# A two-layer hybrid decoder trunk on one core: first x ahead of the first weights, turns of y a pair later, other banks for the auxiliary tiles, casts behind scalings at a seam

## The chip, the core and the metric

The kernel runs on one core of a Trainium2 chip. The metric is the device time of one execution in microseconds, here the median of the runs. The profile comes from one further execution, taken by the hardware profiler. The engines are TensorE (PE in the profile; PEld is its weight load, the load of the stationary operand, which overlaps the matmuls), VectorE (DVE), ScalarE (ACT), GpSimd (POOL) and SyncE (SP), whose queue issues most of the DMA transfers.

## The reference

Two layers over 256 tokens of width 2048, all in float32. Layer 0 has one input projection of 12,336 columns, shared by an mLSTM group (8 heads) and a Mamba-2 SSD group (32 heads of 64); layer 1 is block-sparse attention, which with 256 tokens and blocks of 256 is causal attention over all. Each layer ends in a SwiGLU FFN of width 5632.

```python
def swiglu(x, w_gate, w_up, w_down):
    return (jax.nn.silu(x @ w_gate) * (x @ w_up)) @ w_down

for layer in range(DEPTH):
    xn = rms_norm(x, norm_mix[layer])
    if layer % 2 == 0:
        x = x + mixer_mlstm_ssd(xn, *mixer_params[layer])
    else:
        x = x + mixer_moba(xn, *mixer_params[layer])
    x = x + swiglu(rms_norm(x, norm_ffn[layer]), *ffn_params[layer])
return rms_norm(x, final_norm)
```

Inside `mixer_mlstm_ssd` the SSD group runs a depthwise convolution and SiLU over x, B and C, a chunked scan, and a gated group norm: `y = rms_norm(y * silu(z))` for each of the 8 groups of 256 columns. That y goes with the mLSTM output through one output projection.

## The kernel before

**Products.** Every weight matrix streams once from HBM through SBUF. A float32 product is computed as three float32r products: each operand is cut into a high part (a cast, `wh`, on ScalarE, line 252) and a low part (the difference, `wl`, on VectorE, line 257), and TensorE adds high x high, high x low and low x high (lines 288 to 290) into PSUM. "A product" below means one of these three matmuls of 128 x 512.

**Blocks and pairs.** `block` computes a tile of 256 tokens by 1024 columns. It walks over pairs of 128 contraction rows: 8 pairs for a width of 2048. For each pair, SP loads two raw tiles of 512 KB, ScalarE casts them and VectorE takes the differences. A pair marked P in the table `PLAN` takes 24 products into four accumulators `acc_f` (banks 0 to 3), in the order 0, 2, 1, 3. A pair marked S takes seven Strassen-like sums of three products, 21 instead of 24; four of the sums go into `acc_e` (banks 4, 5, 6 and 7, in the order of use: E1 in 4, E7 in 5, E5 in 6, E6 in 7). The text calls E5 the third and E6 the fourth Strassen sum. Before an S pair VectorE also builds sums of the weights, and of the activations (`sk`, from a copy `xg` of the turned activations).

**Turns.** The activations have to stand with the contraction along the partitions. A turn is four 128 x 128 transposes on TensorE into one auxiliary bank (`transpose_split`, tile `p_tr`, line 209), which ScalarE and VectorE then read to write the high and low parts. The auxiliary tiles take the banks of the list `AUX` in rotation, begun anew at each block; they share banks 4 to 7 with the Strassen sums.

**Order.** Programs for the five engines come from a scheduler that follows program order and priorities (`high_priority`) and explicit ties (`tied`, `issue_after`: an instruction may not be placed ahead of another). Small work between the products is put on a list with `later(wait, ...)` and is run `wait` pairs on, by `tick` at the end of each pair.

**Names that the change touches.** `warm_up` runs matmuls on a tile of ones at the start; `WARM` gives the calls before the turn of the first gains (`p_rows`) and after the turns of the first x (line 413). `load_x` issues the transfers of the input (`xin`, line 107), `first_pair` those of the first weights (line 407). `weights` ties its casts behind the last cast, the last difference and whatever stands in the list `also`. `bc_done` empties the accumulators of a B/C block: `scaled` (line 467) multiplies each by the norm's root into `tok`. `xz_block` (four of them, columns of x and z) does the same, and between its products the scan of the groups before it runs: `p_xs`, `p_y` (line 708), then `ssd_gate`: y is gated, squared and summed, its root is taken on GpSimd (`rrg`, line 137), ScalarE scales y (line 727), and a turn of y (line 209) is set for later. `decay_rows` (line 637) issues transfers on GpSimd's queue. The order of the blocks is: two B/C blocks, four xz blocks, the mLSTM's blocks and the output projection, the FFN of layer 0 ("a", its hidden tiles named `ha`), attention, the FFN of layer 1 ("b", `hb`).

The turns of y before:

```python
for t in range(NT):
    nc.scalar.activation(y[:, t, cs], y[:, t, cs], AF.Copy, scale=rr[:, t:t + 1])
later(1, ("sx", 2 * s + g), transpose_split, sx, 2 * s + g, [y[:, t, cs] for t in range(NT)], G_SS)
```

Of the kernel before, what the change touches and what calls it, by code (L numbers as in the profile page):

```python
# [17 lines left out]
P = 128  # L18
# [13 lines left out]
C_Q, C_K, C_V, C_O, C_I, C_F, C_Z, C_X, C_B, C_C, C_DT = (  # L32
    0, 1024, 2048, 4096, 6144, 6152, 6160, 8208, 10256, 11280, 12304)

WARM = (7, 8)
SPACE = {"raw": 6, "sum": 2, "wh": 6, "wl": 6, "xa": 8, "sk": 3, "s": 9, "vh": 2}
PLAN = {
    "bc": "PPPPPPPP", "xz": "PPPPPPPP", "qk0": "PPPPPPPP", "w1": ("PSPSPSPP", "PSPSPSPP"),
# [23 lines left out]
def hybrid_trunk(ctx: ExitStack, tc: tile.TileContext, a: dict, out: bass.AP):  # L62
# [25 lines left out]
    def tiny(shape, tag):  # L88
        return sml.tile(shape, F32, tag=tag, name=tag, bufs=2)

    turn = [0]
    AUX = (6, 7, 4, 5)

    def bank(i, name):
        return psm.tile([P, 512], F32, tag=f"b{i}", name=name)
# [3 lines left out]
        return bank(AUX[(turn[0] - 1) % len(AUX)], name)  # L99

    ones = cst.tile([P, P], F32, name="ones")
    nc.gpsimd.memset(ones, 1.0)
    xin = [big.tile([P, D], F32, tag="xr", name=f"xin{t}", bufs=2) for t in range(NT)]

    def load_x(lo, n):
        for t in range(NT):
            nc.sync.dma_start(xin[t][:, lo:lo + n], x_in[t * P:(t + 1) * P, lo:lo + n])

    load_x(0, T)
    rows = cst.tile([P, P], F32, name="rows")  # L110
    by_row = lambda nm: a[nm].rearrange("(a b) -> a b", b=P)
    ident = cst.tile([P, P], F32, name="ident")
# [37 lines left out]
            stack.enter_context(tc.issue_after(ins))  # L150
        return stack

    also = []
    last, cast, nth, fresh = [None], [None], [None], [None, None]
    clock = [0]
    held = [False]
# [13 lines left out]
    def tick():  # L170
        clock[0] += 1
        run_until(lambda p: held[0] or p[0] > clock[0])
# [31 lines left out]
    def transpose_split(kt, j, src, gcol):  # L204
        b = kt.pair(j)
        pt = aux_bank("p_tr")
        for i in range(2):
            for t in range(NT):
                turned = nc.tensor.transpose(pt[:, i * T + t * P:i * T + (t + 1) * P], src[t][:, i * P:(i + 1) * P], ident)  # L209
        pair = pt.rearrange("p (a b) -> p a b", a=2)  # L210
        gains = None if gcol is None else [pv[:, gcol + 2 * j + i:gcol + 2 * j + i + 1] for i in range(2)]
        if j in kt.sums:
            xg = t2([P, 2, T], "xg")
            if gains is None:
                nc.scalar.copy(xg, pair)
            else:
                for i in range(2):
                    nc.scalar.activation(xg[:, i, :], pair[:, i, :], AF.Copy, scale=gains[i])
            split(b[:, :, 0, :], b[:, :, 1, :], xg)
            kt.sums[j] = activation_sums(xg, kt.sum_home[j])  # L220
        elif gains is None:
            split(b[:, :, 0, :], b[:, :, 1, :], pair)
        else:
            for i in range(2):
                split(b[:, i, 0, :], b[:, i, 1, :], pair[:, i, :], gains[i])
        return turned.ins
# [52 lines left out]
    def block(src, kt, row, plan, after_sums=None, lead=1, ready=None, order=(0, 2, 1, 3),  # L279
              first_weights=None):  # L280
        n = len(plan)
        F = [None] * 4
        pre = None
        E = {}

        def add(dst, a, b, start, stop, **kw):
            (ah, al), (bh, bl) = a, b
            nc.tensor.matmul(dst, ah, bh, start=start, stop=False, **kw)  # L288
            nc.tensor.matmul(dst, ah, bl, start=False, stop=False, **kw)  # L289
            nth[0] = nc.tensor.matmul(dst, al, bh, start=False, stop=stop, **kw).ins  # L290

        first_s, last_s = plan.find("S"), plan.rfind("S")
        turn[0] = 0
        group = []
        for j in range(n):
            if plan[j] == "S":
                sk = kt.summed(j)
                held[0] = True
                b21, b11, b22, t3, t1, t2_, t4 = weights(src, row + 2 * j * P, True)
                tok = lambda k, t: tuple(x[:, t * P:(t + 1) * P] for x in kt.parts(k))  # L300
                k2, k1 = 2 * j, 2 * j + 1
                a11, a12, a22 = tok(k1, 0), tok(k2, 0), tok(k2, 1)
                s1, s2, s3, s4 = [(sk[:, i, 0, :], sk[:, i, 1, :]) for i in range(4)]
                prod = {1: (a11, b11), 2: (a12, b21), 3: (s4, b22), 4: (a22, t4),
                        5: (s1, t1), 6: (s2, t2_), 7: (s3, t3)}
                for p in (2, 1, 3, 7, 5, 6, 4):
                    if p in (2, 3, 4):
                        i = p - 2
                        fresh = F[i] is None
                        if fresh:  # L310
                            F[i] = bank(i, "acc_f")
                        add(F[i], *prod[p], start=fresh, stop=False)
                    else:
                        if p not in E:
                            E[p] = bank({1: 4, 7: 5, 5: 6, 6: 7}[p], "acc_e")
                        add(E[p], *prod[p], start=j == first_s, stop=j == last_s)
                if j == last_s:
                    pre = [t2([P, STRIP], "pre") for _ in range(4)]
                    p1, v, u3, w = pre
                    with tc.high_priority(offset=1600):  # L320
                        nc.scalar.copy(p1, E[1])
                        nc.vector.tensor_add(v, p1, E[6])
                        nc.vector.tensor_add(u3, v, E[7])
                        nc.vector.tensor_add(v, v, E[5])
                        nc.vector.tensor_add(w, u3, E[5])
                    if after_sums is not None:
                        after_sums(pre)
            else:
                group.append((j, first_weights if j == 0 and first_weights else weights(src, row + 2 * j * P, False)))
                if ready is not None:  # L330
                    ready(j, False)
                if len(group) < lead and j < n - 1 and n - j <= lead:
                    continue
                for i in order:
                    t, s = divmod(i, 2)
                    first = F[i] is None
                    if first:
                        F[i] = bank(i, "acc_f")
                    halves = (slice(0, T), slice(T, STRIP)) if lead > 1 and j == n - 1 and i == order[-1] else (slice(0, STRIP),)
                    for cs in halves:  # L340
                        apart = cs.start > 0
                        if apart:
                            F.append(bank(4, "acc_last"))
                        dst = F[4][:, :T] if apart else F[i][:, cs]
                        for jj, w in group:
                            for kk in range(2):
                                xh, xl = kt.parts(2 * jj + kk)
                                ts = slice(t * P, (t + 1) * P)
                                add(dst, (xh[:, ts], xl[:, ts]), [v[:, cs] for v in w[s][kk]],
                                    start=(first or apart) and jj == group[0][0] and kk == 0,  # L350
                                    stop=jj == n - 1 and kk == 1)
                    if ready is not None and i == 2:
                        with tc.issue_after(nth[0]):
                            ready(j, True)
                group = []
            tick()
            if j == last_s:
                held[0] = False
        return F, pre
# [104 lines left out]
    def scaled(t, src, r):  # L464
        d = t2([P, STRIP], "tok")
        with tc.high_priority(offset=1600):
            nc.scalar.activation(d, src, AF.Copy, scale=r[:, t:t + 1])  # L467
        return d

    def bc_done(s, got):  # L470
# [157 lines left out]

    settled.close()
    later(2, "gates", gate_chain)  # L630
    later(6, "gates", gate_columns)

    def decay_rows(first, home):
        need("gates")
# [14 lines left out]


    FB = bc_block(1)
    also.clear()
    bc_done(1, FB)

    sx = KT("sx", KD, s_home, {1: vh_home, 3: vh_home, 5: sk_home})
# [62 lines left out]
    def ssd_gate(s, g, y, zg):  # L718
        cs = slice(g * T, (g + 1) * T)
        nc.vector.tensor_mul(y[:, :, cs], y[:, :, cs], zg[:, :, cs])  # L720
        ssg = tiny([P, NT], "ssg")
        for t in range(NT):
            sumsq(ssg[:, t:t + 1], y[:, t, cs])
        rr = tiny([P, NT], "rrg")
        rsqrt_mean(rr, ssg, T)
        for t in range(NT):
            nc.scalar.activation(y[:, t, cs], y[:, t, cs], AF.Copy, scale=rr[:, t:t + 1])
        later(1, ("sx", 2 * s + g), transpose_split, sx, 2 * s + g, [y[:, t, cs] for t in range(NT)], G_SS)

    for s in range(4):  # L730
        xz_block(s)
# [315 lines left out]
    def finish_last(F):  # L1047
# [17 lines left out]
            dve(nc.vector.tensor_scalar, so_far[t], so_far[t], 1.0 / D, EPS, op0=OP.mult, op1=OP.add)  # L1065

        def root(t, n):
            rf[t] = tiny([P, 1], "rf")
            dve(nc.vector.scalar_tensor_tensor, rf[t], ssf[t][:, n:n + 1], 1.0 / D, so_far[t], op0=OP.mult, op1=OP.add)
            with tc.high_priority(offset=1600):  # L1070
                nc.gpsimd.tensor_tensor(rf[t], rf[t], mhalf[:, :1], op=OP.pow)

        def scale(t, cs, queue, on_scalar=False):
            x = xr_[t]
# [59 lines left out]
```

## Time and profile before

| what | value |
|---|---|
| median of 3 runs | 2576.79 us (2576.51 to 2577.45) |
| the profiled execution | 2576.37 us, span 2574.6 us |
| granted TensorE clock, mean of the span | 0.999 |
| TensorE busy | 2558.9 us, 99% of the span |
| VectorE, ScalarE, GpSimd busy | 87%, 58%, 2% |
| DMA | 494.52 MB, 192 GB/s on average |

The timeline's rows give the start, the busy time, the engine, the line, the operation, what it writes and reads, and in brackets how long the engine stood before it and for what. A product's row has 0.39 us, but products are pipelined: what counts is the distance from one start to the next. "PE p_tr L209 <- ACT y L727: 2.9, 5, 0.7" in the list of waits says that matmuls of the tile p_tr of line 209 waited five times for the ScalarE instruction of line 727 on y, 2.9 us in all and 0.7 at the longest.

### The profile page before, as it was taken

What the parts mean: (1) busy time and instruction counts of PE and PEld (TensorE: products, weight loads), DVE (VectorE), ACT (ScalarE), POOL (GpSimd) and SP (SyncE); (2) the same over time, 40 slices, a digit from 0 to 9 for tenths busy, and PEclk for the clock granted to TensorE, in tenths of its full rate; (3) what the DMA queues carried; (4) which work ended last, traced back from release to release, by engine and by line L of the source; (5) the groups of instructions that cost most, each with busy time, mean ns of one, the idle gap of its engine ahead of it and who ended that gap; (6) DMA issues with size and microseconds to landing.
All of it is one profiled execution on the core that took longest, in us unless ns stands there. A gap on an engine that the chain in (4) does not pass through costs nothing.

```text
span 2574.6 us, 32831 instructions
## 1 busy us (share of the span) xinstructions
PE 2558.9 (99%) x11699; PEld 2110.6 (82%) x11699; DVE 2238.3 (87%) x3027; ACT 1504.7 (58%) x2032; POOL 63.6 (2%) x106
## 2 busy tenths in 40 slices
PE   9999999999999999999999999999999999999998
PEld 7888888888888888888888888888888888888887
DVE  5777789877799999999999988978899999999998
ACT  6566666565666555555555655656565555554554
POOL 2001110000000000000000000000000000000000
PEclk9999999999999999999999999999999999999999
DMA  8556666656566666665666656555556666656664
GB/s 270 171 175 181 189 172 206 198 176 212 164 193 190 204 188 214 188 212 182 218 186 207 193 184 193 176 164 179 176 176 197 194 205 191 204 189 228 195 203 142
DMA packets 255699, 494.52 MB, mean 192 GB/s; under 512 B 16120, under 2 KB 18688, under 8 KB 255536
## 3 DMA queue, kind: packets, MB, share of 16 engines
q1 hardware_dynamic: 251088, 482.08, 59.8%
q0 software_dynamic: 3264, 8.51, 1.5%
q8 instruction: 92, 1.51, 0.2%
q10 hardware_dynamic: 1184, 1.84, 0.2%
q14 instruction: 71, 0.58, 0.1%
HBM read 490.23 MB, written 2.14 MB: 191 GB/s over the span
## 4 chain that ended last, share of the span: by engine, by line
PE 93%; issue 4%; POOL 1%; DVE 1%; ACT 0%; DMA 0%; SPq 0%; POOLq 0%; DVEq 0%; ACTq 0%
PE acc_f L288 25%; PE acc_f L290 25%; PE acc_f L289 25%; PE acc_e L288 5%; PE acc_e L290 5%; PE acc_e L289 5%; PE p_tr L209 1%; POOL rows L637 0%; PE p_qt L753 0%; PE p_num L796 0%; PE p_o L1010 0%; PE p_qk L982 0%; PE p_y L708 0%; PE p_pt L1001 0%; DVE wl L257 0%
## 5 line engine op out<-in xcount | busy, mean ns | idle before, releaser
L252 ACT CAST wh<-raw 128x1024 fp32r<-128x1024 f32 (+1 forms) x1038 | 1023.1, 999 | 830.6 <-PE acc_f L290 578.2
L257 DVE TENSOR_TENSOR wl<-raw,wh 128x1024 fp32r<-128x1024 f32 (+1 forms) x1038 | 1186.8, 1155 | 233.3 <-ACT wh L252 231.3
L288 PE MATMUL acc_f<-wh,x 128*128 128x512 f32 x1336 | 524.1, 392 | 0.0
L290 PE MATMUL acc_f<-wh,x 128*128 128x512 f32 x1336 | 521.5, 390 | 0.0
L289 PE MATMUL acc_f<-wl,x 128*128 128x512 f32 x1336 | 521.3, 390 | 0.0
L290 PEld LDWEIGHTS acc_f<-wh,x 128*128 128x128 f32 x1336 | 250.8, 188 | 52.2
L289 PEld LDWEIGHTS acc_f<-wl,x 128*128 128x128 f32 x1336 | 251.2, 188 | 51.2
L288 PEld LDWEIGHTS acc_f<-wh,x 128*128 128x128 f32 x1336 | 250.9, 188 | 50.9
L288 PE MATMUL acc_f<-wh,xa 128*128 128x512 f32 x708 | 281.8, 398 | 0.7 <-ACT tok L467 0.7
L290 PE MATMUL acc_f<-wh,xa 128*128 128x512 f32 x708 | 277.6, 392 | 0.0
L289 PE MATMUL acc_f<-wl,xa 128*128 128x512 f32 x708 | 276.8, 391 | 0.0
L257 DVE TENSOR_TENSOR wl<-sums,wh 128x1024 fp32r<-128x1024 f32 x128 | 156.1, 1220 | 11.9 <-ACT wh L252 11.9
L290 PEld LDWEIGHTS acc_f<-wh,xa 128*128 128x128 f32 x708 | 133.2, 188 | 28.0
L288 PEld LDWEIGHTS acc_f<-wh,xa 128*128 128x128 f32 x708 | 133.4, 188 | 26.4 <-ACT tok L467 0.9
L289 PEld LDWEIGHTS acc_f<-wl,xa 128*128 128x128 f32 x708 | 133.3, 188 | 26.2
L288 PE MATMUL acc_e<-wh,sk 128*128 128x512 f32 x384 | 152.7, 398 | 0.0
L289 PE MATMUL acc_e<-wl,sk 128*128 128x512 f32 x384 | 150.1, 391 | 0.0
L290 PE MATMUL acc_e<-wh,sk 128*128 128x512 f32 x384 | 149.9, 391 | 0.0
L252 ACT CAST wh<-sums 128x1024 fp32r<-128x1024 f32 x128 | 134.0, 1047 | 21.0 <-PE acc_f L290 10.5
L367 DVE TENSOR_TENSOR pre<-pre,acc_f 128x512 f32<-128x512 f32 x152 | 102.6, 683 | 6.3 <-PE acc_f L290 4.0
L288 PE MATMUL acc_f<-wh,ha 128*128 128x512 f32 x262 | 102.4, 391 | 0.0
L290 PE MATMUL acc_f<-wh,ha 128*128 128x512 f32 x262 | 102.0, 389 | 0.0
(339 smaller groups left out, 3725.1 us busy)
## 6 DMA issues: line engine op xcount, KB each, us to landing
raw<-in_l_w_in SPq DMA_DIRECT2D x192, 512.0 KB, 4.2
raw<-in_l_ffn_gate SPq DMA_DIRECT2D x176, 512.0 KB, 4.4
raw<-in_l_ffn_up SPq DMA_DIRECT2D x176, 512.0 KB, 4.4
raw<-in_l_ffn_down SPq DMA_DIRECT2D x176, 512.0 KB, 4.8
raw<-in_l_w_qkv SPq DMA_DIRECT2D x96, 512.0 KB, 4.4
raw<-in_l_w_out SPq DMA_DIRECT2D x64, 512.0 KB, 4.6
raw<-in_l_w_o SPq DMA_DIRECT2D x32, 512.0 KB, 3.8
rows<-scr POOLq DMA_DIRECT2D x20, 256.0 KB, 5.5
```

The source lines that it names most:

```text
L209: turned = nc.tensor.transpose(pt[:, i * T + t * P:i * T + (t + 1) * P], src[t][:, i * P:(i + 1) * P], ident)
L252: cast[0] = nc.scalar.copy(h[:, :n, :], of[:, :n, :]).ins
L257: last[0] = nc.vector.tensor_sub(l[:, :n, :], of[:, :n, :], h[:, :n, :].bitcast(F32)).ins
L288: nc.tensor.matmul(dst, ah, bh, start=start, stop=False, **kw)
L289: nc.tensor.matmul(dst, ah, bl, start=False, stop=False, **kw)
L290: nth[0] = nc.tensor.matmul(dst, al, bh, start=False, stop=stop, **kw).ins
L367: nc.vector.tensor_add(pre[i], pre[i], F[i])
```

## The change

Eight edits, the last without effect on the order:

1. The second warm-up has 4 calls instead of 8.
2. `AUX` begins with bank 7, then 6.
3. The memset of ones and the first transfer of x get a high priority.
4. The transposes of a turn are tied behind the last product placed so far (`nth[0]`).
5. At the block behind one whose accumulators are scaled (`scaled`), the weights of the third pair are tied behind the last scaling (`evacuated`), and the ties in `also` end with the first pair of that block instead of its last.
6. The gates' columns are set seven pairs on instead of six.
7. The turns of y are set two pairs on instead of one.
8. The last norm's mean has a tile of its own.

```diff
-WARM = (7, 8)
+WARM = (7, 4)
...
-    AUX = (6, 7, 4, 5)
+    AUX = (7, 6, 4, 5)
...
-    nc.gpsimd.memset(ones, 1.0)
+    with tc.high_priority(offset=4000):
+        nc.gpsimd.memset(ones, 1.0)
...
-    load_x(0, T)
+    with tc.high_priority(offset=4000):
+        load_x(0, T)
...
-    also = []
+    also, evacuated = [], []
...
         pt = aux_bank("p_tr")
-        for i in range(2):
-            for t in range(NT):
-                turned = nc.tensor.transpose(...)
+        with tied(nth[0]):
+            for i in range(2):
+                for t in range(NT):
+                    turned = nc.tensor.transpose(...)
...
             else:
+                if j == 2 and evacuated:
+                    also[:] = evacuated
                 group.append((j, first_weights if j == 0 and first_weights else weights(src, row + 2 * j * P, False)))
...
                 group = []
+            if ready is None and evacuated:
+                also.clear()
             tick()
...
         with tc.high_priority(offset=1600):
-            nc.scalar.activation(d, src, AF.Copy, scale=r[:, t:t + 1])
+            evacuated[:] = [nc.scalar.activation(d, src, AF.Copy, scale=r[:, t:t + 1]).ins]
...
-    later(6, "gates", gate_columns)
+    later(7, "gates", gate_columns)
...
     FB = bc_block(1)
-    also.clear()
...
-        later(1, ("sx", 2 * s + g), transpose_split, sx, 2 * s + g, [y[:, t, cs] for t in range(NT)], G_SS)
+        later(2, ("sx", 2 * s + g), transpose_split, sx, 2 * s + g, [y[:, t, cs] for t in range(NT)], G_SS)
...
-            rf[t] = tiny([P, 1], "rf")
-            dve(nc.vector.scalar_tensor_tensor, rf[t], ssf[t][:, n:n + 1], 1.0 / D, so_far[t], op0=OP.mult, op1=OP.add)
+            rf[t], mean = tiny([P, 1], "rf"), tiny([P, 1], "mean_f")
+            dve(nc.vector.scalar_tensor_tensor, mean, ssf[t][:, n:n + 1], 1.0 / D, so_far[t], op0=OP.mult, op1=OP.add)
             with tc.high_priority(offset=1600):
-                nc.gpsimd.tensor_tensor(rf[t], rf[t], mhalf[:, :1], op=OP.pow)
+                nc.gpsimd.tensor_tensor(rf[t], mean, mhalf[:, :1], op=OP.pow)
```

The rows below are the scheduled order of an engine's instructions (line, operation, what it writes and reads, shape, how many in a row). The changed kernel's lines stand a few lines further down: 107, 209, 252, 407, 467 and 708 become 108, 212, 255, 414, 474 and 714.

SP's queue at the start of the program, before (xin are the tiles of the input, raw the weights):

```order
L407 DMA raw<-in_l_w_in 128x2x512 x2
L107 DMA xin_78<-in_x 128x256
L107 DMA xin_79<-in_x 128x256
L107 DMA xin_78<-in_x 128x256
L107 DMA xin_79<-in_x 128x256
```

And after:

```order
L108 DMA xin_78<-in_x 128x256
L108 DMA xin_79<-in_x 128x256
L414 DMA raw<-in_l_w_in 128x2x512 x2
L108 DMA xin_78<-in_x 128x256
L108 DMA xin_79<-in_x 128x256
```

The first two transfers of x have moved ahead of the two first weight transfers; what follows them stays. On GpSimd's queue the memset of ones has moved ahead of one of a weight tile.

ScalarE at the seam between the first and the second block, before (xa are the turned inputs of the first block's last pair, tok the scalings, rb a copy for the gates):

```order
L144 ACTIVATE xa_444<-p_tr,pv 128x256 x2
L252 CAST wh<-raw 128x1024 x6
L467 ACTIVATE tok<-acc_f,r_544 128x512 x4
L521 COPY rb_555<-p_rb 128x256
L252 CAST wh<-raw 128x1024 x2
```

And after:

```order
L146 ACTIVATE xa_440<-p_tr,pv 128x256 x2
L255 CAST wh<-raw 128x1024 x4
L474 ACTIVATE tok<-acc_f,r_540 128x512 x4
L255 CAST wh<-raw 128x1024 x2
L528 COPY rb_551<-p_rb 128x256
```

Two of the six casts have moved behind the four scalings. On VectorE one difference (line 257) has moved behind dg (line 518), and on TensorE p_rb now stands ahead of the turn p_rows.

TensorE in the second xz block, at a turn of y, before (xa_444 are the inputs of a pair; the products go on above and below):

```order
L288 MATMUL acc_f<-wh,xa_444 128x512
L289 MATMUL acc_f<-wl,xa_444 128x512
L209 MATMUL p_tr<-ident,y 128x128
L290 MATMUL acc_f<-wh,xa_444 128x512
L288 MATMUL acc_f<-wh,xa_444 128x512
```

And after, at the same turn (xa_440 is the pair that was xa_444, the block's last; xa_107 belongs to the next block's first):

```order
L292 MATMUL acc_f<-wl,xa_440 128x512
L293 MATMUL acc_f<-wh,xa_440 128x512
L212 MATMUL p_tr<-ident,y 128x128 x4
L291 MATMUL acc_f<-wh,xa_107 128x512
L292 MATMUL acc_f<-wl,xa_107 128x512
```

Before, this turn's first transpose stood inside the pair, 10 products ahead of its end, and the other three 3 products into the next one (in other places the two parts stood 1 to 6 products apart); now all four stand together at the end of the pair. The p_y from which this y comes has moved ahead by 14 products, to the end of a pair, so 48 products lie between it and the turn where 24 lay. The other turn of a block now stands right behind that p_y. On GpSimd's queue, in each xz block, two transfers of decay rows (line 637) that stood between two roots (line 137) now stand ahead of both. In the FFN blocks the eight transposes of a turned hidden tile stand as before, two and then six with one product triple between; in the six down blocks that follow a hidden block, and in two of attention, the fourth Strassen sum now stands ahead of the third. One turn of the last hidden group of FFN "a" stands 13 products later.

More of the change, by code (lines that the diff above doesn't have):

```diff
@@ L206, in transpose_split @@
         pt = aux_bank("p_tr")
-        for i in range(2):
-            for t in range(NT):
-                turned = nc.tensor.transpose(pt[:, i * T + t * P:i * T + (t + 1) * P], src[t][:, i * P:(i + 1) * P], ident)
+        with tied(nth[0]):
+            for i in range(2):
+                for t in range(NT):
+                    turned = nc.tensor.transpose(pt[:, i * T + t * P:i * T + (t + 1) * P], src[t][:, i * P:(i + 1) * P], ident)
         pair = pt.rearrange("p (a b) -> p a b", a=2)
```

## The prediction

> **What bounds the kernel now.** I read the page's totals first, then the chain that ended last, then the list of waits of TensorE, and last the timeline at the places which those waits name.
>
> ```profile
> PE 2558.9 (99%) x11699; PEld 2110.6 (82%) x11699; DVE 2238.3 (87%) x3027; ACT 1504.7 (58%) x2032; POOL 63.6 (2%) x106
> ...
> PE 93%; issue 4%; POOL 1%; DVE 1%; ACT 0%; DMA 0%; SPq 0%; POOLq 0%; DVEq 0%; ACTq 0%
> ```
>
> TensorE is busy 99% of the span and carries 93% of the chain. The change leaves the number and the order of the products as they are, so it can only win what TensorE loses between them. The waits of the matmuls, and below them those of the weight loads:
>
> ```profile
> PE p_tr L209 <- ACT y L727: 2.9, 5, 0.7
> ...
> PE acc_f L288 <- ACT tok L467: 0.7, 1, 0.7
> ...
> ```
>
> ```profile
> PEld acc_e L288 <- DVE ha L142: 4.5, 11, 0.4
> PEld acc_e L288 <- DVE hb L142: 4.5, 11, 0.4
> ...
> PEld p_y L708 <- DVE rows L693: 0.9, 3, 0.4
> ```
>
> Columns: total us, how many, the longest. Three places stand out, and each has a part of the change: the turns of y, the seam at line 467, and 22 weight loads of a Strassen bank; the fourth part is at the start. The 9.0 us of these loads are not all lost, since a load runs beside the matmul before it.
>
> **Part 1, first x ahead of first weights, and a shorter second warm-up.** The start, in the order of the timeline (start, us, engine, line):
>
> ```profile
> 0.74 0.94 SPq L407 DMA_DIRECT2D raw<-in_l_w_in  x2
> ...
> 1.74 2.27 SPq L107 DMA_DIRECT2D xin<-in_x  x4
> ...
> 5.62 0.20 PE L124 MATMUL p_rows<-ident,rows 16*128 16x16 f32 x1 [0.59 <-DMA rows<-in_l_norm_mix]
> ...
> 6.91 0.33 PE L413 MATMUL p_tr<-ident,xin 128*128 128x128 f32 x1 [1.10 <-DMA xin<-in_x]
> ...
> 7.80 3.14 PE L118 MATMUL warm<-ones 128*128 128x128 f32 x16
> ...
> 8.00 0.47 ACT L144 ACTIVATE xa<-p_tr,pv 128x256 fp32r<-128x256 f32 x1 [4.77 <-PE p_tr L413]
> ...
> 9.02 0.69 DVE L142 TENSOR_TENSOR wl<-raw,wh 128x512 fp32r<-128x512 f32 x1
> ...
> 10.59 0.77 PE L288 MATMUL acc_f<-wh,xa 128*128 128x512 f32 x1
> ...
> 11.21 1.05 ACT L252 CAST wh<-raw 128x1024 fp32r<-128x1024 f32 x1 [0.17 <-DMA raw<-in_l_w_in]
> ...
> 12.29 2.51 DVE L257 TENSOR_TENSOR wl<-raw,wh 128x1024 fp32r<-128x1024 f32 x2 [0.35 <-ACT wh L252]
> ...
> 13.73 0.39 PE L290 MATMUL acc_f<-wh,xa 128*128 128x512 f32 x1
> ...
> 13.96 0.60 PE L209 MATMUL p_tr<-ident,xin 128*128 128x128 f32 x4
> ...
> 14.63 0.40 PE L289 MATMUL acc_f<-wl,xa 128*128 128x512 f32 x1
> ...
> 17.17 0.39 PE L288 MATMUL acc_f<-wh,xa 128*128 128x512 f32 x1
> ```
>
> The product at 17.17 is the first of the second weight pair: 24 products and one turn earlier stands the one at 10.59. A product at full speed takes 0.227 us from start to start (17.17 is 11 products after 14.63, 2.54/11 = 0.23). The turn costs 14.63 - 13.73 - 2 x 0.227 = 0.45 us.
>
> Issued about 1 us earlier, x lands at 5.9 or before, so the four transposes run right behind p_rows, 5.85 to 6.6. Before, the first product's operands came 1.0 us after the transposes (from 8.00, when xa is begun, to 9.02, when the cast wh is there and wl is begun) and the second's 1.7 us (wl, to 9.71); the 16 warm-up instructions (8 calls in two passes) held TensorE to 10.59. Now the operands are there at 7.7 and 8.4, and 8 warm-up instructions end between 7.5 and 8.2 (8 x 0.196 = 1.6 at the rate of the row). The first product starts at about 7.9, 2.7 us earlier. The two first weight transfers land up to 0.7 us later behind 256 KB of x; their casts follow the transposes anyway.
>
> Not all of the 2.7 arrives, or more. The clock decides:
>
> ```profile
> 5.00:10.00 5.00, 3.14 (x19) 2.86 (x19) 1.64 (x4) 1.95 (x5) 2.65 (x7) 0.83 1.00 315
> 10.00:15.00 5.00, 5.00 (x24) 4.25 (x24) 4.39 (x6) 3.55 (x6) 0.00 (x0) 0.83 1.05 389
> ```
>
> Stretch, length, busy us of PE, PEld, DVE, ACT and POOL, then the granted clock, the DMA share and GB/s. Two neighbouring stretches lose 0.17 x 5 us each: some 3.4 us at half speed, about 8.3 to 11.7, after a stretch in which TensorE was busy 3.14 us of 5. If that half-speed time stays where it was, nine products pass from 7.9 to 11.7 and fifteen and the turn after it (15 x 0.227 + 0.45 = 3.9): second pair at 15.6, a gain of 1.6. At full clock it is 7.9 + 24 x 0.227 + 0.45 = 13.8, a gain of 3.4, and there the weights of the second pair wait: landed 11.2 (unchanged, the same bytes go before them), cast and difference to 13.5. The busy share ahead of 8.3 rises (no idle for x), which the trace can't price; I take the middle, 2.5, and 1.6 and 4 as the ends. Nothing downstream holds the earlier work back: the DMA engines are at their full share (1.05), but the third pair's weights are needed only 5.9 us after the second's.
>
> [...]
>
> **Part 2, casts behind the scalings at the seam between the first two blocks.**
>
> ```profile
> 57.92 0.39 PE L290 MATMUL acc_f<-wh,xa 128*128 128x512 f32 x1
> ...
> 58.40 1.04 ACT L252 CAST wh<-raw 128x1024 fp32r<-128x1024 f32 x1 [1.67 <-PE acc_f L290]
> ...
> 59.35 1.84 ACT L467 ACTIVATE tok<-acc_f,r 128x512 f32<-128x512 f32 x3
> ...
> 60.08 0.50 PE L288 MATMUL acc_f<-wh,xa 128*128 128x512 f32 x1 [0.74 <-ACT tok L467]
> ...
> 60.42 0.39 PE L289 MATMUL acc_f<-wl,xa 128*128 128x512 f32 x1
> ```
>
> ScalarE stood 1.67 us before a cast whose buffer was not free, with the scalings that empty the accumulators queued behind it. With four casts ahead instead of six (none waits for this buffer), the scalings run as the accumulators close. From 57.92 to 60.42 go 2.50 us, less two products 2.05; the p_rows turn and p_rb (5 instructions at about 0.11) need 0.55. Gain 1.5. On VectorE one weight difference now stands behind dg, which p_rb reads, and not ahead of it. The moved casts belong to the third pair, needed 48 products (10.9 us) into the block, against four scalings of 0.6 in front: no cost. At the later seams the list shows no wait, so nothing is won there.
>
> **Part 3, turns of y one pair later, kept together.** One of the five waits, with the rows that lead to it:
>
> ```profile
> 195.06 0.73 POOL L137 TENSOR_TENSOR rrg<-rs,mhalf 128x2 f32<-128x2 f32 x1 [79.23 <-DVE rs L136]
> ...
> 195.75 1.47 POOL L637 DMA_DIRECT2D rows<-scr  x2
> ...
> 205.16 1.00 DVE L693 SCALAR_TENSOR_TENSOR rows<-rows,cols,cb 128x128 f32<-128x128 f32 x3
> ...
> 212.40 0.39 PE L289 MATMUL acc_f<-wl,xa 128*128 128x512 f32 x1
> ...
> 212.89 0.51 ACT L727 ACTIVATE y<-y,rrg 128x256 f32<-128x256 f32 x1 [0.80 <-POOL rrg L137]
> ...
> 213.45 0.33 PE L209 MATMUL p_tr<-ident,y 128*128 128x128 f32 x1 [0.66 <-ACT y L727]
> ...
> 213.85 0.40 PE L288 MATMUL acc_f<-wh,xa 128*128 128x512 f32 x1
> ```
>
> One transpose and two products take 213.85 - 212.40 = 1.45 where 0.45 + 0.11 would do: 0.9 lost for 0.66 listed. Five waits with 2.9 listed make 2.9 x 0.9/0.66 = 4.0. Waits of p_y (0.9 of loads, three times) and turns cut in two add at most 1.5, at least nothing; I take 0.8, since not every cut is paid for. Gain 4.8. In the order this first transpose now stands 10 products later, at the end of its pair, so it is asked for at 212.63 + 2.27 = 214.9; the other three stand 3 products earlier, beside it. The first half of y was scaled at 213.40, and the second half follows one cast of 1.0 later, at 214.9 at the latest. That alone would just do. But p_y, from which y comes, stands 14 products (3.2 us) earlier too, so that 48 products lie between it and the turn; if it really runs there, 3.2 us of room are left. It can if its decay rows come: GpSimd issued them at 195.75, right behind a root (line 137) that had stood in its queue until 195.06 for another y, and VectorE had them ready at 206.16. Now these two issues stand ahead of both roots of the block, with the issues of the other rows, which the queue gave out long before (79 us of idle time at 195.06); only their buffer can hold them.
>
> **Part 4, the auxiliary banks.** In a hidden block of the first FFN, right after the eight transposes of the h before it (start, us, engine, line):
>
> ```profile
> 873.51 0.59 ACT L215 COPY xg<-p_tr 128x512 f32<-128x512 f32 x1
> ...
> 874.65 0.68 DVE L142 TENSOR_TENSOR ha<-p_tr,ha 128x512 fp32r<-128x512 f32 x1
> ...
> 875.01 0.40 PE L290 MATMUL acc_e<-wh,sk 128*128 128x512 f32 x1
> ...
> 875.39 0.50 PE L288 MATMUL acc_e<-wh,sk 128*128 128x512 f32 x1
> ...
> 875.72 0.40 PE L289 MATMUL acc_e<-wl,sk 128*128 128x512 f32 x1
> ```
>
> The third Strassen sum (bank 6) starts when VectorE has read the first turn (bank 6) at 875.33; 875.01 to 875.72 is 0.71 where 0.45 would do: 0.26, and with the product after it 0.28. The second turn (bank 7) is copied by ScalarE at 874.10, 1.1 us before the third sum is due. With the two banks exchanged the third sum finds its bank free, and the fourth (0.68 us later, at 875.9) the other one. This holds where the second turn is copied by ScalarE: 16 of the 22 places, the hidden blocks that follow another one. In the six down blocks VectorE reads both turns late, and the order puts the fourth sum ahead of the third there, so the stall stays. 16 x 0.28 = 4.5; ends 0 (it moves to the fourth sum) and 6.2 (22 x 0.28).
>
> The columns of the gates a pair later, mean_f, and one turn of the last group 13 products later touch nothing that TensorE waits for: 0.
>
> **Sum.** 2.5 + 1.5 + 4.8 + 4.5 = 13.3. The profiled execution took 2576.4 (span 2574.6); the median of the runs is 2576.8. So 2563.1 for the first and 2563.5 for the median.
>
> **Rivals.**
> - The bank stall only changes place: VectorE reads the first turn later than 875.33, and the fourth sum waits instead. Against it: 0.6 us of room in the row. Time 2568.0.
> - The turns of y still wait, as p_y's rows are the new bound or ScalarE reaches the second half late: 2568.3. For it: without earlier rows the room is 0.
> - The start gives nothing, as weights and half clock set it: 2566.0, by the row of 11.21 at least 1.6 is there.
> - The change doesn't do what it says: the turns of h stay cut two and six in the order, so "grouped" is worth nothing there; I count nothing for it. With banks and y both void, 2572.8, the same within a measurement (0.2%, 5 us, is about what can be told).
> - Slower: the buffer of the fourth rows of a block comes free late, so GpSimd holds its issue, with both roots behind it, and p_y, now 3.2 us earlier, waits on TensorE for the rows in each of the four xz blocks. The other parts give 8.5, so it decides from 2.1 us a block; with rows no earlier than before it is 3.2 and the roots' two issues, 1.5, on top: 2576.8 - 8.5 + 4 x 4.7 = 2587.1. For it: the rows took from 195.75 to 206.16. Against: at 195.75 they were issued without a wait.
>
> **Chances.** The forecast with its own range (2560.5 to 2566) 0.58; banks 0.10; y 0.12; start 0.08; two or more void 0.07; slower 0.05. The range from 2559 (start 4, y 5.5, all 22 stalls) to 2569.5 takes the first four. Faster by over 0.2% 0.89, within 0.06, slower 0.05.
>
> **What would show it.** Line 727 gone from TensorE's waits; ha and hb down from 22 loads to six; no wait for tok at line 467; xin x2 as SP's first row and the second pair before 15.7. The forecast fails if a new name of over 3 us stands in TensorE's waits, or if the clock of 10 to 15 us falls below 0.8.

## The result and the profile after

The changed kernel takes 2560.99 us (median of 4 runs, 2560.78 to 2561.11); the kernel before took 2577.12 in 4 runs (2576.51 to 2578.52). The ratio is 0.9937, with a 95% interval of 0.9919 to 0.9954. The profiled execution's span fell from 2574.6 to 2559.3 us, by 15.3, where 13.3 was forecast; the median came out 2.5 us below the forecast of 2563.5, inside its own range (2560.5 to 2566) and 0.5 above the lower end.

The page's first lines and its chain, after:

```profile
span 2559.3 us, 32817 instructions
## 1 busy us (share of the span) xinstructions
PE 2549.0 (100%) x11691; PEld 2111.9 (83%) x11691; DVE 2236.8 (87%) x3027; ACT 1501.9 (59%) x2032; POOL 62.1 (2%) x106
...
PE 98%; DVE 1%; issue 0%; DMA 0%; ACT 0%; POOL 0%; SPq 0%; POOLq 0%; DVEq 0%; ACTq 0%
```

The waits of the matmuls after, all of them (total us, how many, the longest):

```profile
PE warm L120 <- POOL ones L103: 1.0, 1, 1.0
PE acc_f L291 <- ACT wh L143: 0.9, 1, 0.9
PE p_cols L632 <- ACT colsrc L622: 0.4, 1, 0.4
```

And those of the weight loads that answer to ha and hb before:

```profile
PEld acc_e L291 <- DVE hb L144: 1.2, 3, 0.4
PEld acc_e L291 <- DVE ha L144: 1.2, 3, 0.4
```

The turns of y, the scalings at the seam and the first x are gone from the list. One wait is new: the first product stands 0.9 us for the cast of its weights. The 22 loads behind a turn of a hidden tile are 6.

Where the time went can be read off the products themselves, since all kernels here run the same 10,572 in nearly the same order. I counted them in the traces and took the start of the n-th product, minus that of the kernel before (us; negative is earlier):

| products started | place | before | changed | banks_only | y_later_only | x_first | casts_only |
|---|---|---|---|---|---|---|---|
| 24 | second pair | 17.17 | -3.72 | -0.24 | -0.45 | -3.28 | +0.61 |
| 186 | ahead of the seam | 56.79 | -3.64 | -0.24 | -0.45 | -3.06 | +0.62 |
| 200 | behind the seam | 62.03 | -5.12 | -0.23 | -0.44 | -3.06 | -0.86 |
| 576 | ahead of the first turns of y | 163.14 | -5.11 | -0.17 | -0.40 | -3.01 | -0.79 |
| 1536 | behind the xz blocks | 421.20 | -10.46 | +0.06 | -5.85 | +0.53 | -0.75 |
| 3000 | ahead of FFN a | 776.50 | -10.48 | +0.06 | -5.85 | +0.53 | -0.75 |
| 6000 | behind FFN a | 1475.03 | -12.89 | -2.18 | -5.82 | +0.54 | -0.77 |
| 7500 | ahead of FFN b | 1856.08 | -12.91 | -2.10 | -5.70 | +0.58 | -0.67 |
| 10571 | the last | 2566.44 | -15.27 | -4.39 | -5.68 | +0.55 | -0.58 |

The changed kernel's column gives the four parts: start 3.7, seam 1.5, xz blocks 5.35 (from 5.11 to 10.46), FFN blocks 2.4 each. Nothing moves elsewhere.

The start after, from the timeline:

```profile
0.74 0.86 SPq L108 DMA_DIRECT2D xin<-in_x  x2
...
1.65 0.94 SPq L414 DMA_DIRECT2D raw<-in_l_w_in  x2
...
4.49 0.24 PE L126 MATMUL p_rows<-ident,rows 16*128 16x16 f32 x1
...
4.66 0.66 PE L420 MATMUL p_tr<-ident,xin 128*128 128x128 f32 x4
...
5.16 1.06 PE L120 MATMUL warm<-ones 128*128 128x128 f32 x8
...
6.44 0.62 ACT L143 CAST wh<-raw 128x512 fp32r<-128x512 f32 x1 [0.60 <-DMA raw<-in_l_w_in]
...
7.11 0.73 PE L291 MATMUL acc_f<-wh,xa 128*128 128x512 f32 x2 [0.89 <-ACT wh L143]
...
8.40 0.40 PE L291 MATMUL acc_f<-wh,xa 128*128 128x512 f32 x1
8.40 0.19 PEld L292 LDWEIGHTS acc_f<-wl,xa 128*128 128x128 f32 x1
8.63 0.40 PE L292 MATMUL acc_f<-wl,xa 128*128 128x512 f32 x1
...
13.46 0.39 PE L291 MATMUL acc_f<-wh,xa 128*128 128x512 f32 x1
```

The eight warm-up instructions took 0.13 us each and the products stand 0.23 us apart from 8.17 on: full speed, where the first three of before began 0.57 and 0.43 apart. The bound of the start is now the transfer of the first weights, for which ScalarE waited 0.60. The second pair begins at 13.46, before at 17.17.

The seam after. Three of the four scalings run while the last pair's products go on, the fourth right behind them, and the next block's first product follows p_rows at once:

```profile
53.35 0.69 ACT L474 ACTIVATE tok<-acc_f,r 128x512 f32<-128x512 f32 x1 [0.39 <-PE acc_f L293]
...
54.28 0.39 PE L293 MATMUL acc_f<-wh,xa 128*128 128x512 f32 x1
54.51 0.60 PE L526 MATMUL p_rb<-dg,ones 128*128 128x128 f32 x4
...
54.95 0.27 PE L542 MATMUL p_rows<-ident,rows 128*128 128x128 f32 x1
54.98 0.47 PE L291 MATMUL acc_f<-wh,xa 128*128 128x512 f32 x1
...
55.29 1.99 ACT L255 CAST wh<-raw 128x1024 fp32r<-128x1024 f32 x2
```

The same turn of y as in the prediction, on GpSimd, ScalarE and TensorE, with the issue of its block's decay rows:

```profile
106.33 5.81 POOL L644 DMA_DIRECT2D rows<-scr  x8
...
204.06 0.70 POOL L139 TENSOR_TENSOR rrg<-rs,mhalf 128x2 f32<-128x2 f32 x1 [13.41 <-DVE rs L138]
...
204.79 0.51 ACT L733 ACTIVATE y<-y,rrg 128x256 f32<-128x256 f32 x1 [1.74 <-POOL rrg L139]
206.14 0.51 ACT L733 ACTIVATE y<-y,rrg 128x256 f32<-128x256 f32 x1
...
209.44 0.60 PE L212 MATMUL p_tr<-ident,y 128*128 128x128 f32 x4
```

All eight issues of this block's rows run together and end at 112, where the last two were issued at 195.75 before (in the three later blocks the last two moved from 249 to 209, from 302 to 261 and from 355 to 313); y is ready at 206.65, 2.8 us before its turn.

A hidden block after (the counterpart of 873 to 876 before):

```profile
862.73 0.59 ACT L218 COPY xg<-p_tr 128x512 f32<-128x512 f32 x1
...
863.86 0.69 DVE L144 TENSOR_TENSOR ha<-p_tr,ha 128x512 fp32r<-128x512 f32 x1
...
864.23 0.39 PE L293 MATMUL acc_e<-wh,sk 128*128 128x512 f32 x1
...
864.45 0.39 PE L291 MATMUL acc_e<-wh,sk 128*128 128x512 f32 x1
...
865.13 0.39 PE L291 MATMUL acc_e<-wh,sk 128*128 128x512 f32 x1
```

The third Strassen sum starts 0.22 us after the product before it, while VectorE is still reading the other turn (to 864.55), and the fourth at 865.13.

### The profile page after: what moved, and what is told of

It reads as the page before. It is cut to its first block, busy times and chain, and to the rows that moved or that the text cites. A ratio compares the mean times of both kernels' runs of the same rounds, so it can differ in the third digit from the quotient of the medians.

```text
span 2559.3 us, 32817 instructions
## 1 busy us (share of the span) xinstructions
PE 2549.0 (100%) x11691; PEld 2111.9 (83%) x11691; DVE 2236.8 (87%) x3027; ACT 1501.9 (59%) x2032; POOL 62.1 (2%) x106
## 4 chain that ended last, share of the span: by engine, by line
PE 98%; DVE 1%; issue 0%; DMA 0%; ACT 0%; POOL 0%; SPq 0%; POOLq 0%; DVEq 0%; ACTq 0%
PE acc_f L291 26%; PE acc_f L293 26%; PE acc_f L292 26%; PE acc_e L291 5%; PE acc_e L293 5%; PE acc_e L292 5%; PE p_tr L212 2%; PE p_y L714 1%; PE p_qt L759 0%; PE p_num L802 0%; DVE wl L260 0%; PE p_o L1016 0%; PE p_cv L454 0%; PE p_qk L988 0%; PE p_pt L1007 0%
## 5 line engine op out<-in xcount | busy, mean ns | idle before, releaser
L291 PE MATMUL acc_f<-wh,ha 128*128 128x512 f32 x262 | 102.3, 391 | 0.0
L292 PE MATMUL acc_f<-wl,ha 128*128 128x512 f32 x262 | 102.2, 390 | 0.0
```

## The experiments

The theory was that each part takes away its own wait and that the four add up. The rivals were that a wait only changes its place or that one part's gain depends on another.

**The banks alone** (`banks_only`).

```diff
-    AUX = (6, 7, 4, 5)
+    AUX = (7, 6, 4, 5)
```

> The kernel before with the list of auxiliary banks as in the change, and nothing else. If the banks bring what the prediction says, the weight loads of a Strassen sum that wait for line 142 fall from 22 to 6, and the profiled span is 4.5 us shorter (16 x 0.28). If the stall only changes place, 22 loads still wait, now at the fourth sum, and the span is the same within 0.5 us. If the two sums of the down blocks are free too, no load waits and 6.2 us go.

Median 2572.66 against 2577.24 (ratio 0.9984, interval 0.9975 to 0.9992). The loads of a Strassen sum that wait for the read of a turned hidden tile (line 142):

```profile
PEld acc_e L288 <- DVE ha L142: 1.2, 3, 0.4
PEld acc_e L288 <- DVE hb L142: 1.2, 3, 0.4
```

Six are left, and the table gives 2.24 + 2.29 = 4.5 us for the two FFNs. The stall did not move to the fourth sum.

**The turns of y alone** (`y_later_only`).

```diff
-        later(1, ("sx", 2 * s + g), transpose_split, ...)
+        later(2, ("sx", 2 * s + g), transpose_split, ...)
```

> The kernel before with the turns of y set two pairs on, and nothing else. The order already shows all turns of y in one piece, without the tie of edit 4. If the later turn is what counts, the five waits for line 727 go and the span is 4.8 us shorter (ends 4.0 and 5.5). If part of the gain of the xz blocks comes from the other edits (an earlier start, other banks), the waits go but less than 4.0 us is won. If p_y now waits for its rows, a wait of p_y for line 693 of over 1 us stands in its place.

Median 2570.85 (0.9975, 0.9966 to 0.9984). No matmul waits for line 727 or for the decay rows, and the xz blocks are 5.85 - 0.40 = 5.45 us shorter, 5.35 in the changed kernel. The part needs none of the others.

**The first x alone, with the long warm-up** (`x_first`).

```diff
-    nc.gpsimd.memset(ones, 1.0)
+    with tc.high_priority(offset=4000):
+        nc.gpsimd.memset(ones, 1.0)
...
-    load_x(0, T)
+    with tc.high_priority(offset=4000):
+        load_x(0, T)
```

> The kernel before with the memset of ones and the first x ahead, and the second warm-up still of 8 calls. In the changed kernel the 8 warm-up instructions took 0.13 us each from 5.16 on, and the first product stood 0.89 us for a cast that was done at 7.1. If the order of the transfers is what counts, 16 instructions end at 5.16 + 16 x 0.13 = 7.3, and the second pair starts 3.5 us earlier than before, as with the shorter warm-up. If the shorter warm-up counts, the 16 instructions run at 0.2 us as before and end at 8.4, and the second pair starts 2.3 us earlier.

Median 2574.04 (0.9987, 0.9978 to 0.9996). The second pair starts 3.28 us earlier; the changed kernel's, with half the warm-up, 3.72. So the order of the transfers makes nearly all of it. The profiled execution (2576.92, the longest of the runs) lost 3.6 us again near 310 us, which is not the start's doing; it is told in the last section.

**The casts alone** (`casts_only`).

```diff
-    also = []
+    also, evacuated = [], []
...
+                if j == 2 and evacuated:
+                    also[:] = evacuated
...
+            if ready is None and evacuated:
+                also.clear()
...
-            nc.scalar.activation(d, src, AF.Copy, scale=r[:, t:t + 1])
+            evacuated[:] = [nc.scalar.activation(d, src, AF.Copy, scale=r[:, t:t + 1]).ins]
...
-    also.clear()
```

> The kernel before with the casts of the third pair behind the scalings at the seams, and nothing else. If the seam between the first two blocks is all of it, the group of p_rows and p_rb costs 0.6 us in place of 2.07 and the span is 1.5 us shorter. If the other seams gain as well, it is more than 2 us; if the moved casts come too late for the third pair, products wait for line 257 and less than 1 us is won.

Median 2575.64 (0.9994, 0.9985 to 1.0002): by the runs alone not told from no change. The profile tells it: its start was 0.6 us later than before's, and from product 186 to 200 it gained 1.48. At no other seam did it gain or lose more than 0.1.

The four medians lie 4.6, 6.4, 3.2 and 1.6 us below the kernel before, 15.8 together; the change is worth 16.1. Counted by products in the profiled executions the four give 3.3 + 1.5 + 5.4 + 4.5 = 14.7 of 15.3. So the parts add up, and little is left for the rest: edit 4 was run alone (next), edits 6 and 8 were not.

**The tie alone** (`tied_only`), edit 4.

```diff
-        for i in range(2):
+        with tied(nth[0]):
+            for i in range(2):
...
```

> The kernel before with the transposes of a turn tied behind the last product, and nothing else. The order differs only in one turn of the last hidden group of the first FFN (13 products later) and in one exchange in attention; the turns of y stay cut. If grouping by the tie were worth something of its own, the waits for line 727 would shrink; if not, product for product the run lies within 0.3 us of the kernel before, from the start's difference on.

One run, 2578.05, in the range of the kernel before. From the second pair (0.11 us later) to product 1200 (0.15) nothing changes, and the five waits for line 727 are there with 2.9 us. It did not stay within 0.3 us to the end: p_y waited 0.8 us for its rows once, and the run is 1.7 us behind at the end, of which 1.4 arise there, between products 1200 and 1344. Grouping by the tie is worth nothing; the later turn groups by itself.

**The changed kernel with the turns of y one pair on again** (`after_y1`).

```diff
-        later(2, ("sx", 2 * s + g), transpose_split, ...)
+        later(1, ("sx", 2 * s + g), transpose_split, ...)
```

> The changed kernel with the turns of y one pair on, as before. If the parts add up, this costs 5 us (the waits for line 727 come back, 2.9 us of listed idle time with 4 us lost, and the cut turns with 1) and the median lies at 2566. If the earlier start and the free banks have made the waits needless, they don't come back and it is within 1 us of the changed kernel.

Median 2566.47 (ratio to the kernel before 0.996, 0.9946 to 0.9973), 5.5 us above the changed kernel: the waits for y are back with 2.9 us. An earlier start and free banks do not make them needless.

**The changed kernel with the long second warm-up** (`after_warm8`).

```diff
-WARM = (7, 4)
+WARM = (7, 8)
```

> The changed kernel with 8 calls in the second warm-up. If the short warm-up was harmless but not needed, the 16 instructions end at 7.3 at 0.13 us each, and the start is the same within 0.3 us. If it was needed, the first product comes at 8.3 and the second pair over 0.8 us later.

One run, 2561.67. The first product starts at 7.65, held by the warm-up, and the second pair at 13.69, 0.23 after the changed kernel's. The shorter warm-up is worth a few tenths of a microsecond at most. Its size is not shown, since the five profiled kernels with the changed kernel's start have the second pair anywhere from 13.06 to 13.52; both with the long warm-up lie above all five (13.69 here, 13.89 with x first alone).

**The changed kernel with hardly any warm-up** (`after_warm2_1`).

```diff
-WARM = (7, 4)
+WARM = (2, 1)
```

> The changed kernel with 2 and 1 calls of warm-up in place of 7 and 4, so that TensorE is idle for most of the first 7 us. [...] If the warm-ups do nothing for the clock, the second pair starts at 13.5 as in the changed kernel.

One run, 2563.22. The products from 8.05 on and the first ones of the full speed:

```profile
8.05 0.63 PE L293 MATMUL acc_f<-wh,xa 128*128 128x512 f32 x1
8.48 0.63 PE L291 MATMUL acc_f<-wh,xa 128*128 128x512 f32 x1
...
11.47 0.63 PE L293 MATMUL acc_f<-wh,xa 128*128 128x512 f32 x1
11.89 1.04 PE L212 MATMUL p_tr<-ident,xin 128*128 128x128 f32 x4
12.60 0.56 PE L291 MATMUL acc_f<-wh,xa 128*128 128x512 f32 x1
13.00 0.40 PE L292 MATMUL acc_f<-wl,xa 128*128 128x512 f32 x1
13.24 0.40 PE L293 MATMUL acc_f<-wh,xa 128*128 128x512 f32 x1
```

The first product came earlier (6.61), but it and the next ones stand 0.43 us apart up to about 12.6, and the second pair starts at 15.54, 2.1 later than in the changed kernel. Here the missing warm-up cost these 2.1 us, and four calls behind the seven were enough: with eight the second pair came at 13.69, not earlier. Which of the two warm-ups counts was not tried.

**What is left of the bank stall.** Six loads still waited. Two ways to reach them were tried on top of the change.

First another order of the seven sums in a block's first S pair (`after_sorder`):

```diff
-                for p in (2, 1, 3, 7, 5, 6, 4):
+                for p in ((2, 1, 3, 7, 4, 5, 6) if j == first_s else (2, 1, 3, 7, 5, 6, 4)):
```

> The changed kernel with another order of the seven sums in the first S pair of a block: the sum of the accumulator that comes last is put ahead of the third and fourth Strassen sums. So both of those start 0.68 us later, after VectorE has read the turns of the hidden tile (before, the sum came 0.35 us too early). If the stall of the six down blocks is this, their six waits for line 142 go and 1.7 us are won (6 x 0.28). If the accumulator's weights (the last to be made ready, line 257) are not there yet, products of that sum wait, up to 1.2 us in each of 40 S blocks, and the kernel is slower by up to 10 us.

Median 2560.24, 0.75 below the changed kernel (ratio to before 0.9935, 0.9923 to 0.9948). Beyond the first product no matmul waited for weights. But the six waits gave back only part: counted by products, 0.28 is won at each and 0.16 lost some 28 products later. There, in a down block:

```profile
955.32 0.69 DVE L144 TENSOR_TENSOR ha<-p_tr,ha 128x512 fp32r<-128x512 f32 x1
...
955.85 0.39 PE L292 MATMUL acc_f<-wl,ha 128*128 128x512 f32 x1
956.12 0.19 PEld L291 LDWEIGHTS acc_e<-wh,sk 128*128 128x128 f32 x1 [0.31 <-issue]
956.15 0.47 PE L291 MATMUL acc_e<-wh,sk 128*128 128x512 f32 x1
```

VectorE reads the second turn to 956.01 and the last Strassen sum, whose bank this is, follows. TensorE came there 0.28 earlier and now met a limit that it had just missed. The trace names "issue"; the load began 0.1 us after the read had ended.

So the second way was to put VectorE's reads of the turned tile ahead (`after_prio`):

```diff
         elif gains is None:
-            split(b[:, :, 0, :], b[:, :, 1, :], pair)
+            with tc.high_priority(offset=1200):
+                split(b[:, :, 0, :], b[:, :, 1, :], pair)
```

> The changed kernel with a higher priority for the two instructions that read a turned hidden tile from its bank, so that VectorE's read (line 142 before) stands ahead of the weight sums in its order, 0.7 us earlier, and the second read of a down block well before that. If the six stalls that are left come from VectorE's place alone, they go without any other order of the sums: 1.7 us less (6 x 0.28), median 2559.3. If the weights that now stand behind (sums, and the differences at line 257) come late, products wait for them: up to 0.7 us in each of 22 blocks, and the kernel is as fast as before or up to 14 us slower.

Median 2560.03 (0.9932, 0.9918 to 0.9945). Six loads still wait, but 0.2 at the longest and 1.0 in all instead of 2.4; by products the two FFNs are 1.5 us shorter than in the changed kernel, of the 1.7 that were to be had. Its execution lost 0.9 us at the start to one late weight difference.

Both together (`sorder_prio`):

> The changed kernel with both: the higher priority of the reads, and the accumulator's sum ahead of the third and fourth Strassen sums in the first S pair. In the run with the other order alone each of the six stalls of 0.28 went, but 0.16 came back six pairs of products later, where the last Strassen sum waited for VectorE's read of the second turn. If that is what came back, it goes here, and the span is 1.0 us below that run's (6 x 0.16) and 1.7 below the changed kernel's. If the priority alone already does it, this equals the run with the priority within 0.2 us.

Median 2559.06 (0.9929, 0.9916 to 0.9941), 1.9 us below the changed kernel and below every other here. No load waits for a turned hidden tile. The two FFNs are 6.7 us shorter than in the kernel before (3.35 each), where the changed kernel has 4.8 and the order alone 5.5: 1.9 against the first, 0.2 more than the six stalls of 0.28 make up, and 1.2 against the second, where 1.0 was expected for the read of the second turn. The priority alone does not equal it.

## Why the prediction was right

**Direction and place.** The four places read from the waits and the timeline are the four places where the time came from, and each part alone removes its own. No error of one part hid one of another: the seam gave what was forecast and the other three more, 2.0 us in all.

**The banks** (4.5 forecast) gave 4.5 alone and 4.8 in the changed kernel; 16 of 22 loads stopped waiting, and the six that stayed are those of the down blocks. The 0.3 more in the changed kernel was not traced.

**The seam** (1.5) gave 1.48 in both kernels, the changed one and the one with the casts alone.

**The turns of y** (4.8) gave 5.35 to 5.45. The term taken at 0.8 for cut turns and p_y's waits was mis-sized: beside the 4.0 for the five waits it is some 1.4, near the upper end of 1.5. A count over the xz blocks, from the product ahead of each group of small instructions to the second product behind it, less what these products take at full speed, splits the gain. The eight turns cost 7.6 us before and 3.3 after, so 4.2 comes from them, their waits and their cuts together; the groups of p_y and p_xs give 0.7, part of it p_y's waits (0.9 listed at the loads before, none after); the rest is spread. The same 304 small instructions stand at 53 places between products before and at 34 after. The step that p_y's rows would come early enough held: nothing but the root had kept their issue, which moved ahead by some 85 us in the block shown and some 40 in the three others. The room was put at 3.2 us and is 2.8.

**The start** (2.5) gave 3.7 and is the term that was furthest off. It was the middle between 1.6 at half clock and 3.4 at full clock: a choice between two cases, of which the second came. What it took over from the trace, the place of the slow stretch, is not even fixed for the old start: of the five profiled executions with it only the kernel before has slow products, two or three of them, and the other four run their first pair at full speed from 10.7 to 11.7 on. The idle time for x, which the prediction could not price, is gone (1.3 us in the list before, nothing after). All seven profiled executions that have x first and at least four calls in the second warm-up ran their first pair at full speed but for a few products at its head (second pair 13.1 to 13.9); the five with the old start have the second pair at 16.7 to 17.8, so one pair of executions tells the size of this part to within some 0.5 us only. The rival of a half clock did not come; the run with 2 and 1 calls shows that it was real. That its second pair came at 15.54, where I had computed 15.6 for a half clock, is chance: its first product came at 6.61 and not at 7.9, and the slow products lasted to 12.6 and not to 11.7. Its products stand 0.43 us apart there, those of the changed kernel 0.23; the two kernels differ in the warm-up calls alone, and how these come to act on the clock is not shown. Two other numbers of the start were off and worked against each other: p_rows, which I left at 5.62, ran at 4.49, as its own transfer landed earlier (3.2 us behind its issue, 4.3 before), and the first weights landed not 0.7 but 1.4 us later (5.01 in the trace before, 6.4 after, where the cast waits for them), so that the first product had a new wait of 0.89 and started at 7.11, 0.8 before the 7.9 of the forecast.

The rivals that a stall moves (banks), that y goes on waiting, and that the rows hold GpSimd are each excluded by a list of waits, the last one also by the rows of GpSimd above; that "grouped" is worth nothing was right.

## What to carry to other kernels

Where one engine is busy 99% of the time, the list of its waits and the start distances of neighbouring instructions priced three of the four parts here to within 0.7 us (the start, where two transfers changed places, was off by 1.2); price a wait by the distance between the instructions around it, since the listed idle time was 0.66 us where 0.9 was lost (matmuls) and 0.41 where 0.28 was lost (weight loads). When two tiles of different use share a bank, give the earlier of two next users the bank whose reader is done first (16 of 22 loads stopped waiting here), and look for the limit just behind the one that is taken away (with another order of the sums 0.16 of each 0.28 came back). Put transfers ahead of an arithmetic instruction that waits for data: two issues of rows in the queue behind such a root went out here at 195.75, when its wait of 79.23 us was over, and by 112 once they stood ahead of it.

## What the runs showed that was not expected

The clock column missed a slow start in one run here. It showed the slow stretch of the kernel before (0.83 twice, in the rows of the prediction), with a granted clock of 1.00 on both sides of it. For the run with hardly any warm-up, where products stood 0.43 us apart from 7.2 to 12.6, the stretches read (the last three columns are granted clock, DMA share and GB/s):

```profile
5.00:10.00 5.00, 4.33 (x13) 3.31 (x12) 3.41 (x6) 3.13 (x6) 2.66 (x7) 1.00 1.02 327
10.00:15.00 5.00, 5.00 (x19) 4.01 (x19) 1.07 (x2) 2.03 (x4) 0.00 (x0) 1.00 1.06 393
```

13 matmuls in 4.33 busy us tell it (22 in 4.11 in the changed kernel); the 1.00 does not. The first clock record of this trace is at 12.8 us, and ahead of it the column reads 1.00 while the products stand 0.43 us apart.

A transfer on GpSimd's queue landed late enough to matter in one run, and more was lost than the wait: 3.6 us for 2.0. In the run with x first alone:

```profile
299.32 1.46 POOL L639 DMA_DIRECT2D rows<-scr  x2
...
307.43 0.76 DVE L643 TENSOR_TENSOR rows<-rows,mask_sl 128x256 f32<-128x256 f32 x2 [1.92 <-DMA rows<-scr]
...
308.97 0.66 PE L710 MATMUL p_y<-y,rows 128*128 128x64 f32 x4 [1.95 <-DVE rows L695]
309.44 0.56 PE L292 MATMUL acc_f<-wh,xa 128*128 128x512 f32 x1
309.80 0.63 PE L290 MATMUL acc_f<-wh,xa 128*128 128x512 f32 x1
310.23 0.63 PE L291 MATMUL acc_f<-wl,xa 128*128 128x512 f32 x1
```

8.1 us lie between the issue and the first use, and the transfer took as long to land; the same one took 6.1 in the kernel before, where it was issued at 302.4. TensorE lost 3.6 us, but the wait itself only 2.0 of it, counted to the product at 309.44. The other 1.6 is a slow clock behind it: the granted clock from 309.7 to 313.0 reads 0.50, and the products of that stretch stand 0.43 us apart, where those ahead of the wait stand 0.23 apart. Between the last product ahead of the wait and p_y lay 2.3 us. In no other profile here does the clock fall between the start and the last microseconds, but that the stop brought it on is not shown by one run. The run with the tie alone shows a smaller case (0.8 us of p_y's wait). Why these transfers were slow stays open. Such long times to landing still come with the later turn (up to 8.3 us in the run with it alone), but with the rows issued that far ahead no matmul waits for them in any of the profiles that have it.
